# One accumulator and one tail per tile and head group: window and compressed exponentials scaled on POOL by the ratio to the selected branch's factor

## The chip, the cores and the metric

The kernel runs on one core of a Trainium2 chip. The metric is device time in microseconds (us). A core has five engines with a queue each, which run in order and wait for each other through semaphores: PE (matrix products and transposes, which write PSUM), DVE (vector), ACT (activation functions and copies), POOL (vector work without access to PSUM) and SP (which only issues DMAs here).

## The reference, cut to what matters

A decoder layer: RMS norm, one input projection, a token mixer of eight attention heads beside a short convolution, an output projection, then a squared-ReLU MLP. All of it is float32, 1024 tokens of 1024 features. The attention has three branches over the same queries, and each has its own softmax:

```
p_cmp = masked_softmax(q.k_cmp - slope * dist)   # 63 compressed keys
p_slc = masked_softmax(q.k_slc - slope * dist)   # all earlier keys (16 of 16 blocks are taken)
p_win = masked_softmax(q.k_win - slope * dist)   # the last 512 keys
o = g0 * (p_cmp @ v_cmp) + g1 * (p_slc @ v_slc) + g2 * (p_win @ v_win)   # g: sigmoid gates
```

masked_softmax divides by the row's sum. With e for the exponentials, branch b contributes f_b * (e_b @ v_b), where f_b = gate_b / sum_b is one number for each query and head.

## The kernel before

Tokens stand in 8 tiles of 128 (`tb`), heads in 2 groups (`g`) of 4. The attention stage goes over the tiles in the order 3, 2, 1, 0, 4, 5, 7, 6 and in each over both groups: 16 rounds. A round has two parts.

`scores(tb, g, ...)` makes for each head the score products (PE, two matmuls a piece, since float32 values are split in a high and a low part), adds the distance penalty and takes the maximum (DVE, from PSUM), and takes exponentials with their sums (ACT). The exponentials of a head lie in one tile `pt`: the first 640 columns hold the window's (WW = min(128 * (tb + 1), 640) of them are in use), the others the selected branch's. The compressed exponentials of all four heads lie in `pc`, 256 columns. `sm` holds the sums by branch and head, and `rr` becomes the factors f_b: a DVE product with `gates` (which holds 1 + exp(-z), the gate's reciprocal) and a reciprocal. `HEADS` is the order of the heads, and a head's place in it is `sl`.

`weigh(tb, g, ...)` returns steps, which the next round's `scores` runs between its heads (`filler`). A step is a block of 128 keys: `load` transposes the exponentials of four heads to PSUM (tile `tp`) and splits them into `ph` (ACT) and `pl` (DVE), `use` multiplies them with the values (`vs`, `vw`, or `vc` and `vco`) into an accumulator `ot`. At the last block of a branch `tail` takes the accumulator out: ACT copies it to `oTs`, PE transposes it back in four pieces into `ops`, and what follows scales it by `rr[:, b]` and adds it to `og`, a part of the tile's output row `osb`, on POOL. The branches come in the order selected (b = 1, tb + 1 blocks), window (2, at most 5 blocks), compressed (0, one block). `finish` then normalizes `osb`, transposes it (`tpo`) and makes the output projection (`wa`). The tiles `ops`, `tpo` and `wa` share one PSUM bank (tag `ms`), the accumulators two (tag `ot`).

`queries` prepares a tile's queries, with a memset and a cast into `Qz` on POOL, which the score products with the low parts need.

None of this runs in the order in which it is written. All calls are recorded as nodes of a plan, and `Plan.schedule` orders them over the whole kernel by priorities worked out from a table of costs for each engine, then issues each engine's queue in that order. Any edit so gives a new order. All instructions are issued from one helper, line 268, so the profile tells them apart by tiles.

After the attention the MLP's up and down products follow. Their first weights are prepared while the last tiles are at work.

Of the kernel before, what the change touches and what calls it, by code (L numbers as in the profile page):

```python
# [494 lines left out]
def trunk_layer(ctx, tc, x, g_mix_norm, w_in, g_q, g_k, pe_cmp, w_cmp1, b_cmp1, w_cmp2, b_cmp2,  # L495
# [182 lines left out]
    with ExitStack() as b1:  # L678
# [120 lines left out]
        for tb, ps in (a for tbs in QUADS for a in z_tokens(pieces, tbs, 280, steps, 1)):  # L799
            z = zt.tile([P, 512], F32, name="z")  # L800
            copy_act(z[:, :280], ps[:, :280])
            k_norm(z[:, 0:128], 2, kn[tb // 2][:, tb % 2, 1])
            v_split(z[:, 128:256], "w", tb)
            e = st.tile([P, 3 * H], F32, name="ge")
            nc.scalar.activation(e, z[:, 256:280], AF.Exp, scale=-1.0)
            for g in range(G):
                eg = e[:, g * 12:(g + 1) * 12].rearrange("p (i j b) -> p b j i", i=2, b=3)
                nc.vector.tensor_scalar(gates[:, tb, g].rearrange("p b (j i) -> p b j i", j=2), eg, 1.0, None,
                                        op0=ALU.add)

        pieces = w_chunk(0, 512, lo_eng=nc.vector)
        for tb, ps in (a for tbs in QUADS for a in z_tokens(pieces, tbs, 512, steps, 1)):
# [24 lines left out]
    with ExitStack() as b2:  # L837
# [92 lines left out]
        def scores(tb, g, Qt, filler):  # L930
            Qg, Qz = Qt
            W = (tb + 1) * P
            WW = min(W, 640)
            nm = st.tile([P, 3, R], F32, name="nm")
            sm = st.tile([P, 3, R], F32, name="sm")
            pc = pts[g].tile([P, R, NCMP], F32, name="pc", bufs=1)
            Ps = []
            k_w = NCMP + T + W - WW
            N = NCMP + W
            cuts = [N] if N <= 512 else [320, N] if N <= 640 else [N - 512, N] if N <= 1024 else [320, N - 512, N]  # L940
            pieces = []
            c0 = 0
            for c1 in cuts:
                parts = [] if c0 else [(0, 0, NCMP, 0)]
                o = max(c0, NCMP)
                parts.append((1, o - NCMP, c1 - o, o - c0))
                pieces.append((c0, c1 - c0, parts))
                c0 = c1
            if WW == 640:
                pieces.append((k_w + 384, 256, [(2, 384, 256, 0)]))  # L950
                pieces.append((k_w, 384, [(2, 0, 384, 0)]))
            else:
                pieces.append((k_w, WW, [(2, 0, WW, 0)]))
            banks = []
            for k, n, parts in pieces:
                m = max(n, 256)
                for bank in banks:
                    if bank[0] + m <= 512:
                        break
                else:  # L960
                    bank = [0, []]
                    banks.append(bank)
                bank[1].append((k, m, bank[0], parts))
                bank[0] += m
            dtile = {0: (d_c, 56 - 8 * tb), 2: (d_sw, 512 + 640 - WW), 1: (d_sw, T - W)}
            for sl, r in enumerate(HEADS):
                sc = -(2.0 ** -(g * R + r + 1))
                pt = pts[g].tile([P, 640 + T], F32, name="pt", bufs=R)
                Ps.append(pt)
                dst = {0: pc[:, r], 2: pt[:, 0:WW], 1: pt[:, 640:640 + W]}  # L970
                seen = set()
                for _, group in banks:
                    s_ = psS.tile([P, 512], F32, name="s_")
                    for k, m, s0, _ in group:
                        nc.tensor.matmul(s_[:, s0:s0 + m], Qg[:, r], KH[g][:, k:k + m], start=True, stop=False)
                        nc.tensor.matmul(s_[:, s0:s0 + m], Qz[:, r], KL[:, k:k + m], start=False, stop=True)
                    for k, m, s0, parts in group:
                        for b, off, n, x in parts:
                            dd, d0 = dtile[b]
                            if b == 1 and d0 + off >= 512:  # L980
                                d0 += P
                            acc = nm[:, b, sl:sl + 1]
                            nc.vector.tensor_tensor_reduce(out=dst[b][:, off:off + n], in0=s_[:, s0 + x:s0 + x + n],
                                                           in1=dd[:, d0 + off:d0 + off + n],
                                                           scale=sc, scalar=acc if b in seen else 1e20,
                                                           op0=ALU.add, op1=ALU.min, accum_out=acc)
                            seen.add(b)
                for b in (1, 2):
                    nc.scalar.activation(dst[b], dst[b], AF.Exp, bias=nm[:, b, sl:sl + 1],
                                         scale=-1.0, accum_out=sm[:, b, sl:sl + 1])  # L990
                for _ in range(-(-len(filler) // (R - sl))):
                    filler.pop(0)()
            order = "p (j i) -> p i j"
            mx = nm[:, 0].rearrange(order, j=2).unsqueeze(3).to_broadcast([P, 2, 2, NCMP])
            pv = pc.rearrange("p (i j) n -> p i j n", j=2)
            tt(nc.gpsimd, pv, mx, pv, ALU.subtract)
            nc.scalar.activation(pc, pc, AF.Exp)
            nc.vector.tensor_reduce(sm[:, 0].rearrange(order, j=2), pv, axis=AX.X, op=ALU.add)
            rr = st.tile([P, 3, R], F32, name="rr")
            nc.vector.scalar_tensor_tensor(rr, sm, 1e-30, gates[:, tb, g], op0=ALU.max, op1=ALU.mult)  # L1000
            nc.vector.reciprocal(rr, rr)
            return (Ps, pc), rr

        def queries(tb):
            Qs = []
# [57 lines left out]
    with ExitStack() as c_:  # L1063
# [15 lines left out]
        def weigh(tb, g, probs, rr, osb):  # L1079
# [15 lines left out]
            def use(ot, first, last, ph, pl, vs):  # L1095
# [3 lines left out]
                for i, v in enumerate(vs):  # L1099
                    o = ot[0][:, i * w:(i + 1) * w]  # L1100
                    nc.tensor.matmul(o, v, ph, start=first, stop=False)
                    nc.tensor.matmul(o, v, pl, start=False, stop=last)

            def tail(ot, b):
                oTs = pq.tile([P, 512], F32, name="oTs", bufs=2)
                copy_act(oTs, ot[0])
                ops = psC.tile([P, R, 2, HD], F32, name="ops", tag="ms", bufs=1)
                for r in range(R):
                    nc.tensor.transpose(ops[:, r].rearrange("p a d -> p (a d)"), oTs[:, r * P:(r + 1) * P], ident)
                t = pq.tile([P, R, 2, HD], F32, name="ot_s", bufs=2)  # L1110
                tv = t.rearrange("p (j i) a d -> p j i a d", j=2)
                if b in (0,9):
                    copy_act(t, ops)
                    tt(nc.gpsimd, tv[:, :, :, 0], tv[:, :, :, 0], tv[:, :, :, 1], ALU.add)
                    c = rr[:, b].rearrange("p (j i) -> p j i", j=2).unsqueeze(3).to_broadcast([P, 2, 2, HD])
                    tt(nc.gpsimd, tv[:, :, :, 0], tv[:, :, :, 0], c, ALU.mult)
                    tt(nc.gpsimd, og, og, tv[:, :, :, 0], ALU.add)
                    return
                c = rr[:, b].unsqueeze(2).unsqueeze(3).to_broadcast([P, R, 2, HD])
                tt(nc.vector, t, ops, c, ALU.mult)  # L1120
                if b == 1:
                    tt(nc.gpsimd, og, tv[:, :, :, 0], tv[:, :, :, 1], ALU.add)
                else:
                    for k in range(2):
                        tt(nc.gpsimd, og, og, tv[:, :, :, k], ALU.add)

            def flat(a):
                return a.rearrange("p a d -> p (a d)")
# [2 lines left out]

            def drain(n):
                while len(fifo) > n:
                    ot, first, last, hl, v, b = fifo.pop(0)
                    use(ot, first, last, *hl, v)
                    if last:
                        tail(ot, b)

            def block(ot, first, last, ins, v, b):
                hl = load(ins)  # L1140
                drain(2)
                fifo.append((ot, first, last, hl, v, b))

            def cols_of(o):
                return [p[:, o:o + P] for p in Ps]

            for b, blocks in ((1, [(cols_of(640 + j * P), [flat(V["s"][:, j, g])]) for j in range(tb + 1)]),
                              (2, [(cols_of(j * P), [flat(V["w"][:, tb + 1 - nw + j, g])]) for j in range(nw)]),
                              (0, [([flat(pc[:, 2 * i:2 * i + 2]) for i in range(2)], [v[:, g] for v in VC])])):
                ot = []  # L1150
                for i, a in enumerate(blocks):
                    steps.append(lambda a=(ot, i == 0, i == len(blocks) - 1) + a + (b,): block(*a))
            steps.append(lambda: drain(0))
            return steps

# [380 lines left out]
```

## Time and profile before

| what | value |
|---|---|
| median of 3 runs | 1266.03 us (1264.09 to 1266.17) |
| the profiled execution: time, span | 1264.1 us, 1262.3 us |
| granted PE clock | 0.999 |
| PE, DVE, ACT, POOL busy | 1234.4, 902.1, 683.1, 708.5 us |

The span is what the profiler saw between the first and the last instruction. The busy time of an engine is not what it costs: only work on the chain that ends last sets the time. In the profile, `out<-in` names an instruction by the tiles it writes and reads, and `PEld` is PE's loading of weights, which overlaps its products.

### The profile page before, as it was taken

The numbers are of one execution on the slowest core, as the hardware profiler recorded it, in microseconds if no ns is written. First come the engines' busy times: TensorE is split into PE (matmuls) and PEld (weight loads), VectorE is DVE, ScalarE is ACT, GpSimd is POOL, SyncE is SP. The second block draws the span as 40 slices with busy tenths as digits, with TensorE's granted clock in tenths as the row PEclk, the third lists the DMA queues.
The fourth block names the chain that finished last, engine by engine and source line by source line (L and its number), as shares of the span: only waits on it lengthen the run. The fifth ranks groups of instructions, "written<-read, shape, count | busy, mean of one in ns | idle before, by whom it ended". The sixth has DMA issues, their size and how long they took to land.

```text
span 1262.3 us, 18410 instructions
## 1 busy us (share of the span) xinstructions
PE 1234.4 (98%) x6170; PEld 1023.4 (81%) x6170; DVE 902.1 (71%) x1805; ACT 683.1 (54%) x1418; POOL 708.5 (56%) x631
## 2 busy tenths in 40 slices
PE   7999999999999999999999999999999999999998
PEld 6898888888878888888778888888888787888786
DVE  6367874434787888988785656566558999898874
ACT  7345552111688888887957455554435444444440
POOL 2155522121044532322687777778788989888860
PEclk9999999999999999999999999999999999999999
DMA  6253441213220100000315445354349654544413
GB/s 236 77 126 119 134 118 50 70 38 122 73 76 34 58 28 18 26 18 18 117 65 193 132 153 166 115 171 159 133 150 371 206 173 167 169 154 132 139 42 133
DMA packets 91574, 147.67 MB, mean 117 GB/s; under 512 B 10900, under 2 KB 45800, under 8 KB 91480
## 3 DMA queue, kind: packets, MB, share of 16 engines
q1 hardware_dynamic: 88408, 138.70, 33.1%
q10 hardware_dynamic: 2304, 5.24, 1.1%
q0 software_dynamic: 768, 2.56, 0.6%
q8 instruction: 49, 0.80, 0.3%
q14 instruction: 45, 0.37, 0.1%
HBM read 102.43 MB, written 44.04 MB: 116 GB/s over the span
## 4 chain that ended last, share of the span: by engine, by line
PE 87%; DMA 4%; ACT 4%; DVE 3%; issue 1%; SPq 0%; POOL 0%; ACTq 0%; DVEq 0%; POOLq 0%
PE X L268 24%; PE Z L268 16%; PE zc L268 10%; PE zp L268 8%; PE tp L268 6%; PE ot L268 5%; PE wa L268 4%; PE W L268 3%; PE wc L268 3%; DMA wu<-in_w_up_dram 2%; PE ops L268 1%; DVE we L268 1%; PE hp L268 1%; DVE y L268 1%; ACT wu L268 1%
## 5 line engine op out<-in xcount | busy, mean ns | idle before, releaser
L268 PE MATMUL X<-we,uu 128*128 128x512 f32 x720 | 179.2, 390 | 1.6 <-DVE y L268 1.5
L268 PEld LDWEIGHTS X<-we,uu 128*128 128x128 f32 x720 | 134.5, 188 | 31.5 <-ACT uu L268 2.2
L268 PE MATMUL Z<-we,uu 128*128 128x512 f32 x576 | 146.8, 391 | 0.3 <-DVE y L268 0.3
L268 ACT ACTIVATE uu<-ur 128x512 fp32r<-128x512 f32 x108 | 67.7, 633 | 127.2 <-PE X L268 57.4
L268 PEld LDWEIGHTS Z<-we,uu 128*128 128x128 f32 x576 | 107.3, 188 | 25.2 <-DVE y L268 2.1
L268 POOL TENSOR_TENSOR d<-d 128x512 f32<-128x512 f32 x64 | 97.0, 1536 | 10.0 <-DVE d L268 8.8
L268 PE MATMUL tp<-ident,pt 128*128 128x128 f32 x528 | 101.9, 273 | 0.2 <-DVE rs_t L268 0.2
L268 DVE TENSOR_TENSOR pl<-tp,ph 128x512 fp32r<-128x512 f32 (+1 forms) x148 | 94.5, 655 | 9.2 <-ACT ph L268 7.8
L268 ACT ACTIVATE pt<-pt,nm 128x640 f32<-128x640 f32 (+7 forms) x128 | 94.1, 739 | 8.4 <-DVE nm L268 7.6
L268 ACT ACTIVATE ph<-tp 128x512 fp32r<-128x512 f32 (+1 forms) x148 | 82.3, 579 | 27.9 <-PE tp L268 17.0
L268 ACT ACTIVATE w_hi<-w_raw,cols 128x128 fp32r<-128x128 f32 (+3 forms) x128 | 54.1, 488 | 67.8 <-PE zc L268 48.3
L268 DVE TENSOR_TENSOR y<-X,y 128x512 f32<-128x512 f32 x128 | 79.8, 681 | 13.7 <-PE X L268 13.0
L268 POOL TENSOR_TENSOR uu<-ur,uu 128x512 fp32r<-128x512 f32 x54 | 77.5, 1440 | 13.6 <-DVE y L268 8.8
L268 DVE TENSOR_TENSOR we<-s,we 128x512 fp32r<-128x512 f32 x42 | 40.7, 969 | 56.8 <-ACT we L268 25.4
L268 DVE SCALAR_TENSOR_TENSOR w_lo<-w_raw,cols,w_hi 128x128 fp32r<-128x128 f32 (+3 forms) x128 | 62.3, 530 | 24.4 <-ACT w_hi L268 24.3
L268 DVE TENSOR_TENSOR uu<-ur,uu 128x512 fp32r<-128x512 f32 x54 | 69.2, 1293 | 12.5 <-ACT uu L268 11.4
L268 PEld LDWEIGHTS tp<-ident,pt 128*128 128x128 f32 x528 | 67.8, 140 | 11.8 <-PE s__4915 L268 0.6
L268 DVE TENSOR_TENSOR y<-Z,y 128x512 f32<-128x512 f32 x96 | 61.3, 683 | 21.1 <-PE Z L268 21.1
L268 ACT ACTIVATE we<-wu 128x512 fp32r<-128x512 f32 x57 | 35.8, 634 | 59.8 <-PE X L268 47.8
L268 ACT ACTIVATE wu<-wu,cols 128x256 f32<-128x256 f32 x128 | 55.6, 506 | 22.5 <-DMA wu<-in_w_up_dram 22.1
L268 PE MATMUL zc<-hTl,w_hi 128*128 128x512 f32 x192 | 65.3, 389 | 0.0
L268 PE MATMUL zc<-hTh,w_lo 128*128 128x512 f32 x192 | 65.1, 390 | 0.0
(1270 smaller groups left out, 3596.9 us busy)
## 6 DMA issues: line engine op xcount, KB each, us to landing
u_d<-d SPq DMA_DIRECT2D x112, 256.0 KB, 5.5
ur<-u_d SPq DMA_DIRECT2D x108, 256.0 KB, 2.7
wu<-in_w_up_dram SPq DMA_DIRECT2D x16, 1024.0 KB, 6.1
wd<-in_w_down_dram SPq DMA_DIRECT2D x16, 1024.0 KB, 5.9
w_raw<-in_w_in_dram SPq DMA_DIRECT2D x20, 512.0 KB, 3.9
xt<-in_x_dram SPq DMA_DIRECT2D x10, 512.0 KB, 5.5
w_raw<-in_w_cmp_dram SPq DMA_DIRECT2D x8, 512.0 KB, 3.9
q_d<-qn SPq DMA_DIRECT2D x8, 512.0 KB, 2.9
```

The source lines that it names most:

```text
L268: node.do.append(lambda: getattr(engine, method)(*[real(x) for x in a], **{k: real(x) for k, x in kw.items()}))
```

## The change

There is one accumulator for all three branches, and one tail. Since only one factor can be applied at its end, that of the selected branch, the window's and the compressed exponentials are multiplied beforehand by f_2 / f_1 and f_0 / f_1. POOL does this, in place: two products on 128x4 for the ratios (`rr[:, 2]` and `rr[:, 0]`), four on a head's WW window columns, one on `pc`. The factors themselves now lie in `ra`, which takes the place of `sm`. 1 + exp(-z) is cut off at 1e20 (a second operation of the same instruction) and the sums at .5 where 1e-30 was. The blocks of the three branches form one list, the first starts the accumulator and the last ends it.

```diff
--- before.py
+++ after.py
@@ -805,8 +805,8 @@
             nc.scalar.activation(e, z[:, 256:280], AF.Exp, scale=-1.0)
             for g in range(G):
                 eg = e[:, g * 12:(g + 1) * 12].rearrange("p (i j b) -> p b j i", i=2, b=3)
-                nc.vector.tensor_scalar(gates[:, tb, g].rearrange("p b (j i) -> p b j i", j=2), eg, 1.0, None,
-                                        op0=ALU.add)
+                nc.vector.tensor_scalar(gates[:, tb, g].rearrange("p b (j i) -> p b j i", j=2), eg, 1.0, 1e20,
+                                        op0=ALU.add, op1=ALU.min)
 
         pieces = w_chunk(0, 512, lo_eng=nc.vector)
         for tb, ps in (a for tbs in QUADS for a in z_tokens(pieces, tbs, 512, steps, 1)):
@@ -963,9 +963,11 @@
                 bank[1].append((k, m, bank[0], parts))
                 bank[0] += m
             dtile = {0: (d_c, 56 - 8 * tb), 2: (d_sw, 512 + 640 - WW), 1: (d_sw, T - W)}
+            dst_w = []
             for sl, r in enumerate(HEADS):
                 sc = -(2.0 ** -(g * R + r + 1))
                 pt = pts[g].tile([P, 640 + T], F32, name="pt", bufs=R)
+                dst_w.append(pt[:, 0:WW])
                 Ps.append(pt)
                 dst = {0: pc[:, r], 2: pt[:, 0:WW], 1: pt[:, 640:640 + W]}
                 seen = set()
@@ -997,9 +999,17 @@
             nc.scalar.activation(pc, pc, AF.Exp)
             nc.vector.tensor_reduce(sm[:, 0].rearrange(order, j=2), pv, axis=AX.X, op=ALU.add)
             rr = st.tile([P, 3, R], F32, name="rr")
-            nc.vector.scalar_tensor_tensor(rr, sm, 1e-30, gates[:, tb, g], op0=ALU.max, op1=ALU.mult)
-            nc.vector.reciprocal(rr, rr)
-            return (Ps, pc), rr
+            nc.vector.scalar_tensor_tensor(rr, sm, .5, gates[:, tb, g], op0=ALU.max, op1=ALU.mult)
+            ra = sm
+            nc.vector.reciprocal(ra, rr)
+            for b in (2, 0):
+                tt(nc.gpsimd, rr[:, b], ra[:, b], rr[:, 1], ALU.mult)
+            for sl, r in enumerate(HEADS):
+                o = dst_w[sl]
+                tt(nc.gpsimd, o, o, rr[:, 2, sl:sl + 1].to_broadcast([P, WW]), ALU.mult)
+            c = rr[:, 0].rearrange(order, j=2).unsqueeze(3).to_broadcast([P, 2, 2, NCMP])
+            tt(nc.gpsimd, pv, pv, c, ALU.mult)
+            return (Ps, pc), ra
 
         def queries(tb):
             Qs = []
@@ -1099,30 +1109,19 @@
                 for i, v in enumerate(vs):
                     o = ot[0][:, i * w:(i + 1) * w]
                     nc.tensor.matmul(o, v, ph, start=first, stop=False)
-                    nc.tensor.matmul(o, v, pl, start=False, stop=last)
-
-            def tail(ot, b):
+                    nc.tensor.matmul(o, v, pl, start=False, stop=last and i == len(vs) - 1)
+
+            def tail(ot):
                 oTs = pq.tile([P, 512], F32, name="oTs", bufs=2)
                 copy_act(oTs, ot[0])
                 ops = psC.tile([P, R, 2, HD], F32, name="ops", tag="ms", bufs=1)
                 for r in range(R):
                     nc.tensor.transpose(ops[:, r].rearrange("p a d -> p (a d)"), oTs[:, r * P:(r + 1) * P], ident)
                 t = pq.tile([P, R, 2, HD], F32, name="ot_s", bufs=2)
+                c = rr[:, 1].unsqueeze(2).unsqueeze(3).to_broadcast([P, R, 2, HD])
+                tt(nc.vector, t, ops, c, ALU.mult)
                 tv = t.rearrange("p (j i) a d -> p j i a d", j=2)
-                if b in (0,9):
-                    copy_act(t, ops)
-                    tt(nc.gpsimd, tv[:, :, :, 0], tv[:, :, :, 0], tv[:, :, :, 1], ALU.add)
-                    c = rr[:, b].rearrange("p (j i) -> p j i", j=2).unsqueeze(3).to_broadcast([P, 2, 2, HD])
-                    tt(nc.gpsimd, tv[:, :, :, 0], tv[:, :, :, 0], c, ALU.mult)
-                    tt(nc.gpsimd, og, og, tv[:, :, :, 0], ALU.add)
-                    return
-                c = rr[:, b].unsqueeze(2).unsqueeze(3).to_broadcast([P, R, 2, HD])
-                tt(nc.vector, t, ops, c, ALU.mult)
-                if b == 1:
-                    tt(nc.gpsimd, og, tv[:, :, :, 0], tv[:, :, :, 1], ALU.add)
-                else:
-                    for k in range(2):
-                        tt(nc.gpsimd, og, og, tv[:, :, :, k], ALU.add)
+                tt(nc.gpsimd, og, tv[:, :, :, 0], tv[:, :, :, 1], ALU.add)
 
             def flat(a):
                 return a.rearrange("p a d -> p (a d)")
@@ -1131,25 +1130,25 @@
 
             def drain(n):
                 while len(fifo) > n:
-                    ot, first, last, hl, v, b = fifo.pop(0)
+                    ot, first, last, hl, v = fifo.pop(0)
                     use(ot, first, last, *hl, v)
                     if last:
-                        tail(ot, b)
-
-            def block(ot, first, last, ins, v, b):
+                        tail(ot)
+
+            def block(ot, first, last, ins, v):
                 hl = load(ins)
                 drain(2)
-                fifo.append((ot, first, last, hl, v, b))
+                fifo.append((ot, first, last, hl, v))
 
             def cols_of(o):
                 return [p[:, o:o + P] for p in Ps]
 
-            for b, blocks in ((1, [(cols_of(640 + j * P), [flat(V["s"][:, j, g])]) for j in range(tb + 1)]),
-                              (2, [(cols_of(j * P), [flat(V["w"][:, tb + 1 - nw + j, g])]) for j in range(nw)]),
-                              (0, [([flat(pc[:, 2 * i:2 * i + 2]) for i in range(2)], [v[:, g] for v in VC])])):
-                ot = []
-                for i, a in enumerate(blocks):
-                    steps.append(lambda a=(ot, i == 0, i == len(blocks) - 1) + a + (b,): block(*a))
+            blocks = [(cols_of(640 + j * P), [flat(V["s"][:, j, g])]) for j in range(tb + 1)]
+            blocks += [(cols_of(j * P), [flat(V["w"][:, tb + 1 - nw + j, g])]) for j in range(nw)]
+            blocks.append(([flat(pc[:, 2 * i:2 * i + 2]) for i in range(2)], [v[:, g] for v in VC]))
+            ot = []
+            for i, a in enumerate(blocks):
+                steps.append(lambda a=(ot, i == 0, i == len(blocks) - 1) + a: block(*a))
             steps.append(lambda: drain(0))
             return steps
```

How the new plan stands, at two places. POOL, tile 4, first group. Before, these are the row for the compressed scores (`pc`, subtracted from their maximum), the selected tail's add, two adds of the window's tail, and three steps of the compressed tail:

```order
L268 TENSOR_TENSOR pc<-nm,pc 128x256
L268 TENSOR_TENSOR osb<-ot_s 128x2x2x64
L268 TENSOR_TENSOR osb<-osb,ot_s 128x2x2x64 x2
L268 TENSOR_TENSOR ot_s<-ot_s 128x4x64
L268 TENSOR_TENSOR ot_s<-ot_s,rr 128x4x64
L268 TENSOR_TENSOR osb<-osb,ot_s 128x2x2x64
```

Now, from the ratios on (`rr`), for the same tile and group:

```order
L268 TENSOR_TENSOR rr<-sm,rr 128x4 x2
L268 TENSOR_TENSOR pt<-pt,rr 128x640 x4
L268 TENSOR_TENSOR pc<-pc,rr 128x256
L268 TENSOR_TENSOR osb<-ot_s 128x2x2x64
L268 TENSOR_TENSOR pc<-nm,pc 128x256
L268 COPY Qz<-Qg 64x512
```

The adds of three tails became one (`osb<-ot_s`, which belongs to an earlier round), and the ratios, four products on 640 columns and the one on `pc` stand in one piece, ahead of the next group's `pc` and `Qz`.

PE, around tile 0's last blocks. Before, from the end of a compressed branch (`vco`) on; `s_` are score products of the tile that comes next and `tpq` transposes of its queries:

```order
L268 MATMUL ot<-pl,vco 128x256
L268 MATMUL ops<-ident,oTs 128x128 x4
L268 MATMUL s__4789<-KH_2793,Qg 128x512
L268 MATMUL s__4789<-KL,Qz 128x512
L268 MATMUL tpq<-ident,qx 128x128 x3
L268 MATMUL s__4813<-KH_2793,Qg 128x384
L268 MATMUL s__4813<-KL,Qz 128x384
L268 MATMUL tpq<-ident,qx 128x128
L268 MATMUL tp<-ident,pt 128x128 x2
L268 MATMUL ops<-ident,oTs 128x128 x4
```

Now, in the second group of tile 0; the four `tp<-ident,pt` are its window's transposes, which read what POOL has scaled:

```order
L268 MATMUL tp<-ident,pt 128x128
L268 MATMUL wa<-w_hi,mh 128x512
L268 MATMUL tp<-ident,pt 128x128
L268 MATMUL wa<-w_lo,mh 128x512
L268 MATMUL s__4630<-KH_2793,Qg 128x512
L268 MATMUL tp<-ident,pt 128x128
L268 MATMUL wa<-w_hi,ml 128x512
L268 MATMUL s__4630<-KL,Qz 128x512
L268 MATMUL s__4649<-KH_2793,Qg 128x384
L268 MATMUL tp<-ident,pc 128x128
L268 MATMUL wa<-w_hi,mh 128x512
L268 MATMUL tp<-ident,pc 128x128
```

Before, four `ops` transposes stood behind each branch; now they come once a group, and between the window's transposes stand pieces of an output projection (`wa`) and score products.

## The prediction

> **What bounds the kernel now.** I read the page first: engine shares, slices of the span, and the chain that ended last.
>
> ```profile
> span 1262.3 us, 18410 instructions
> PE 1234.4 (98%) x6170; PEld 1023.4 (81%) x6170; DVE 902.1 (71%) x1805; ACT 683.1 (54%) x1418; POOL 708.5 (56%) x631
> ...
> PE   7999999999999999999999999999999999999998
> ...
> DVE  6367874434787888988785656566558999898874
> ACT  7345552111688888887957455554435444444440
> POOL 2155522121044532322687777778788989888860
> PEclk9999999999999999999999999999999999999999
> ...
> PE 87%; DMA 4%; ACT 4%; DVE 3%; issue 1%; SPq 0%; POOL 0%; ACTq 0%; DVEq 0%; POOLq 0%
> ```
>
> PE is busy in every slice at full clock and carries 87% of the chain; POOL carries none of it. Next the attention stage, the only one that the change touches. The first matmul into an accumulator (view of the tile `ot`) and the last output projection `wa` (chain in order of time) give its ends, so I asked for the busy times of 340 to 640 us (columns: length, then busy time and count of PE, PEld, DVE, ACT, POOL).
>
> ```profile
> L268 PE MATMUL ot<-ph,vs x72: 388/477/504, 339.1 to 609.9; 128*128 128x512 f32 x72
> ```
> ```profile
> 636.26 0.93 PE wa L268 x4
> ```
> ```profile
> 340.00:440.00 100.00, 96.62 (x603) 80.92 (x602) 83.29 (x292) 86.93 (x226) 45.65 (x68) 1.00 0.15 51
> 440.00:540.00 100.00, 97.83 (x619) 83.59 (x618) 88.54 (x291) 82.87 (x174) 33.73 (x52) 1.00 0.08 28
> 540.00:640.00 100.00, 97.66 (x604) 81.27 (x603) 83.11 (x212) 84.00 (x173) 44.41 (x50) 1.00 0.14 48
> sum 300.00, PE 292.12 PEld 245.79 DVE 254.95 ACT 253.80 POOL 123.79; mean PE 97.37 PEld 81.93 DVE 84.98 ACT 84.60 POOL 41.26
> ```
>
> PE is idle for 7.9 us of 300, DVE and ACT for some 45 each, POOL for 176. So PE work taken out here should count nearly in full, as long as nothing new makes PE wait.
>
> The 240 to 260 us stretch is an unbroken run of wide matmuls, and weight loads fill 16.57 of its 20 us, 83%; in the stage they fill 82%. So the stage is nearly as dense by that measure too.
>
> ```profile
> 240.00:260.00 20.00, 20.00 (x90) 16.57 (x89) 7.47 (x9) 4.35 (x6) 8.25 (x6) 1.00 0.25 79
> ```
>
> [...]
>
> **Removed: two of three tails in each of 16 groups** (8 tiles by 2 head groups). The view of the tile `ops` counts them, the one of `ot` the copies, and the chain in order of time (start, duration, piece) gives the rate at which PE issues transposes.
>
> ```profile
> L268 PE MATMUL ops<-ident,oTs x192: 270/272/330, 345.1 to 619.7; 128*128 128x128 f32 x192
> L268 DVE TENSOR_TENSOR ot_s<-ops,rr x32: 675/686/692, 348.9 to 618.5; 128x512 f32<-128x512 f32 x32
> L268 ACT ACTIVATE ot_s<-ops x16: 577/600/663, 354.8 to 620.4; 128x512 f32<-128x512 f32 x16
> ```
> ```profile
> L268 ACT ACTIVATE oTs<-ot x48: 579/599/631, 344.4 to 618.5; 128x512 f32<-128x512 f32 x48
> ```
> ```profile
> 411.77 0.44 PE ops L268 x4
> ...
> 431.08 2.77 PE wa L268 x12
> ...
> 614.43 1.58 ACT wu L268 x4
> ...
> 624.86 2.80 ACT wu L268 x7
> ```
>
> The 272 ns of one transpose overlap the next; four in a row take 0.44 us of the chain, so one costs 0.11 us of PE. 192 become 64: 128 x 0.11 = **14.1 us of PE less**. The matmuls into the accumulator stay as many; only start and stop flags differ. DVE loses 16 x 0.686 = 11.0 us (the window's scaling), ACT 32 x 0.599 + 16 x 0.600 = 28.8 us. Both were under PE, so I cost these at nothing by themselves; they thin out the queues in which the split of transposed exponentials (`ph`, `pl`) stands.
>
> What PE waited for on the old tails is this (engine and tile, releaser: us in total, times, longest):
>
> ```profile
> PEld ops L268 <- ACT oTs L268: 3.9, 10, 0.6
> ...
> PEld tpo L268 <- ACT ot_s L268: 1.7, 3, 1.0
> ...
> PE tpo L268 <- ACT ot_s L268: 1.3, 3, 0.8
> ...
> PE ops L268 <- ACT oTs L268: 1.0, 4, 0.2
> ...
> PE tp L268 <- DVE rr L268: 0.8, 1, 0.8
> ```
>
> Of the 4.9 us on `oTs`, two thirds of the tails go: -3.3 us (bounds 0 and -4.9: a single tail may also be later). The 3.0 us before `tpo` end with ACT's copy of the compressed tail and three POOL steps behind it; the new tail has one DVE scaling and one POOL add. I take half, -1.5 us (bounds 0 and -3.0). Each wait may be counted on both PE rows, so these are upper figures.
>
> **Added and moved on POOL.** Rows of POOL's groups in 340 to 640 us (busy, mean ns):
>
> ```profile
> L268 POOL TENSOR_TENSOR osb<-osb,ot_s 128x256 f32<-128x256 f32 x48 | 37.9, 790 | 23.0 <-DVE ot_s L268 19.6 <-DVE rr L268 1.3
> ...
> L268 POOL TENSOR_TENSOR ot_s<-ot_s 128x256 f32<-128x256 f32 x16 | 11.7, 734 | 3.7 <-ACT ot_s L268 3.5
> L268 POOL TENSOR_TENSOR ot_s<-ot_s,rr 128x256 f32<-128x256 f32 x16 | 9.8, 614 | 0.7
> L268 POOL TENSOR_TENSOR pc<-nm,pc 128x256 f32<-128x256 f32 x15 | 9.2, 615 | 61.3 <-DVE nm L268 48.3 <-DVE rs_t L268 12.7
> ...
> L268 POOL TENSOR_TENSOR wu<-wu 128x512 f32<-128x512 f32 x5 | 6.4, 1285 | 0.2
> L268 POOL TENSOR_TENSOR y<-y,t 128x512 f32<-128x512 f32 x3 | 5.3, 1757 | 0.0
> L268 POOL TENSOR_TENSOR ri<-rs_t,mhalf 128x1 f32<-128x1 f32 x8 | 4.9, 612 | 13.5 <-DVE rs_t L268 12.0 <-DVE rr L268 1.5
> ```
>
> Gone are the first three: 59.4 us. Added per group: two products on 128x4, four on the window's 128xWW, one on `pc`. The row nearest in kind is 128x256 times a broadcast factor, 0.615 us; the step from 256 to 512 columns (734 to 1285 ns) is 2.15 ns a column. So 128 columns 0.34 us, 256 0.615, 384 0.89, 512 1.17, 640 1.44. No row shows 640: proportion to the broadcast row gives 1.54, the slowest row, 1757 ns, 1.44 x 1757/1285 = 1.97; with a start-up of 0.18 us taken off and 1.7 ns a column, 1.27. I take 1.44, the step between two rows of this trace. WW is 128, 256, 384, 512 in tiles 0 to 3 and 640 in the other four: 64 products, 8 x (0.34 + 0.615 + 0.89 + 1.17 + 4 x 1.44) = 70.2 us. `pc`: 16 x 0.615 = 9.8. The 32 small products have no row: 0.61 us (a power on one column, a heavier operation) is above, 0.1 below; I take 0.2, near the start-up, 6.4 us. Together 86 us against 59 removed: POOL goes from 124 to about 151 us of the stage. It stays the idlest engine, so its load by itself costs nothing.
>
> [...]
>
> **The new wait.** The factor needs all three sums of all four heads, so the window's transposes, which used to wait only for their exponentials, now stand behind this chain, and so do the ones of the compressed branch:
>
> ```profile
> L268 ACT ACTIVATE pc<-pc x16: 405/419/436, 329.1 to 600.3; 128x256 f32<-128x256 f32 x16
> L268 DVE TENSOR_REDUCE sm<-pc x16: 407/414/420, 329.7 to 602.2; 128x4 f32<-128x256 f32 x16
> ...
> L268 DVE SCALAR_TENSOR_TENSOR rr<-sm,gates x16: 159/168/690, 332.8 to 604.2; 128x12 f32<-128x12 f32 x16
> L268 DVE RECIPROCAL rr<-rr x16: 211/224/229, 333.0 to 604.9; 128x12 f32<-128x12 f32 x16
> ```
>
> From the last sum: 0.17 + 0.22 on DVE, 2 x 0.2 and four products on POOL: 0.8 us plus 1.4, 2.5, 3.6, 4.7 in tiles 0 to 3 and 5.8 in the larger, so 2.2, 3.3, 4.4, 5.5 and 6.6 us. Behind the waiting transposes on PE stand whatever the planner put there; behind the products on POOL stand the next group's `pc` subtraction and the `Qz` casts, which the next scores need. Cover: the group's own selected blocks come first, and one is four transposes and two matmuls of 0.23 (2.77/12), 0.90 us; there are tb + 1 of them. Own cover alone leaves short 1.3, 1.5, 1.7 and 1.9 us in tiles 0 to 3, and 2.1, 1.2, 0.3, 0 in 4 to 7; twice that, for two groups: 12.8 + 7.2 = 20.0 us. That is the upper bound. The lower is 0: the order quoted ahead shows, in tile 0, output-projection and score matmuls in just that gap, and POOL's products directly behind the ratios. The nearest case in the trace is the old compressed transposes, which hung on the same sums with little behind them to cover: PE's row for that wait (`tp` on `rr`, above) is 0.8 us in the whole stage. I lie nearer to that and take +3 us.
>
> **Sum**, against the profiled execution (1264.1 us, span 1262.3): -14.1 - 3.3 - 1.5 + 3.0 = -15.9, so 1248.2. The median of the runs is 1266.03, 1.9 above that execution: 1250.1, say **1250**. With the bounds: PE's work and all its 7.9 us of idle time gone is -22.0, that is 1244; all 20 us of new waits, no wait saved, is +5.9, that is 1272.
>
> **Rivals.**
> - *New waits take much of it.* Some tiles lack cover, most likely 0 to 3, where 12.8 us are at stake: with a third of the saved waits, -14.1 - 1.6 + 6 to 12.8 gives -9.7 to -2.9, 1256 to 1263. For it: ACT at 87% in 340 to 440 us, so exponentials come late there. Against: the planner orders around it.
> - *Slower: POOL's scaling is held back by DVE.* If each product ran at the 1757/1285 of the slowest POOL row, four on 640 columns would be 7.9 us, the chain 8.7, and own cover would be short by 1.8, 2.4, 3.0 and 3.6 us in tiles 0 to 3 and 4.2, 3.3, 2.4 and 1.5 in 4 to 7, 44 us over both groups. With two thirds of that uncovered: -14.1 - 4.8 + 29.6 = +10.7, 1277. It decides from 19 us of new waits, 1.2 us in each group. Against: DVE's commonest instruction here does not slow, `pl` below.
>
> ```profile
> L268 DVE TENSOR_TENSOR pl<-tp,ph x129: 408/685/694, 345.9 to 599.5; 128x512 fp32r<-128x512 f32 x115, 128x256 fp32r<-128x256 f32 x14
> ```
>
>   Its 685 to 694 ns at 512 columns hold whatever POOL does, for it reads PSUM for one of its inputs, as the score instructions do. [...]
> - *More than the sum.* ACT and DVE, 28.8 and 11 us lighter, also end PE's short waits: -20 to -24, 1242 to 1246.
> - *That it does not do what it says* is excluded for the counts: the order has 64 `ops` transposes. That the gain is given back after the stage I count in the first rival: ACT is on the chain between 614 and 628 us (`wu` above), but 28.8 us lighter ahead of that.
>
> **How the numbers follow.** Likeliest case 0.70 (1246 to 1256), first rival 0.12, slower rival 0.08, more than the sum 0.10. The range from 1244 to 1260 leaves out the slower rival, the upper half of the first and the far end of the last, nearly 2 in 10. A measurement here tells about 0.2%, 2.5 us, from no change; between 1263.5 and 1268.6 I see 0.05, above 0.07, so faster 0.88.
>
> **What would show it.** Right: 64 `ops` transposes, the output projection of the last tile some 15 us earlier, POOL near 150 us in the stage, four products of about 5.8 us in the larger tiles, and few waits of PE on POOL's `pt`. Wrong: PE rows that wait for `pt` from POOL for over 6 us in total, or a POOL product of 640 columns near 2 us. What would make the time wrong even so is PE idle time elsewhere, since every queue is put in a new order.

## The result and the profile after

| kernel | median | ratio to before, 95% interval |
|---|---|---|
| before (same comparison) | 1265.30 us | |
| changed | 1243.98 us (1243.12 to 1246.11, 5 runs) | 0.9837 [0.9823, 0.9852] |

The change makes the kernel 1.63% faster, 20.6 us by the ratio. The forecast was 15.9 us less and 1250 us. The median stands at the low end of the range, 1244 us, below the likeliest case (1246 to 1256 us) and where the rival "more than the sum" had it, with a chance of 0.10. The profiled execution after took 1246.11 us, 18.0 less than the profiled one before, and was the longest of its five.

The page after, rows as shown of before:

```profile
span 1244.2 us, 18122 instructions
...
PE 1217.6 (98%) x6042; PEld 1009.8 (81%) x6042; DVE 890.1 (72%) x1789; ACT 659.2 (53%) x1370; POOL 726.9 (58%) x663
...
PE   7999999999999999999999999999999999999998
...
PEclk9999999999999999999999999999999999999999
...
PE 86%; DMA 6%; DVE 4%; ACT 2%; issue 2%; POOL 0%; SPq 0%; DVEq 0%; ACTq 0%; POOLq 0%
```

PE has 128 instructions less and is as full as before. POOL, with more work, still has no share of the chain. The tile `ops` confirms one tail a group (192 transposes and 32 scalings before):

```profile
L268 PE MATMUL ops<-ident,oTs x64: 270/272/327, 356.3 to 603.6; 128*128 128x128 f32 x64
L268 DVE TENSOR_TENSOR ot_s<-ops,sm x16: 676/685/692, 357.3 to 605.1; 128x512 f32<-128x512 f32 x16
```

I measure the attention stage from the first matmul into `ot` to the last output projection `wa`: 339.1 to 637.9 us before, 341.5 to 619.3 after, so 298.8 and 277.8 us. Whole microseconds of that stretch, before and then after (length, busy time of PE, PEld, DVE, ACT, POOL):

```profile
339.00:638.00 299.00, 291.12 (x1817) 244.91 (x1816) 254.33 (x794) 253.62 (x572) 121.86 (x167) 1.00 0.12 43
```
```profile
342.00:619.00 277.00, 271.39 (x1677) 228.98 (x1677) 240.75 (x776) 229.50 (x523) 133.44 (x191) 1.00 0.14 46
```

The stage is 21 us shorter, and PE's idle time in it fell from 7.9 to 5.6 us. In the second stretch stand 140 PE instructions less, 128 of the tails and 12 others: some lie in the parts of a microsecond at the edges, and a little of the MLP's early work moved behind the stage.

What POOL was given (groups by shape, busy and mean ns):

```profile
L268 POOL TENSOR_TENSOR pt<-pt,rr 128x640 f32<-128x640 f32 x32 | 39.1, 1255 | 0.0
...
L268 POOL TENSOR_TENSOR pc<-pc,rr 128x256 f32<-128x256 f32 x16 | 9.8, 615 | 0.0
...
L268 POOL TENSOR_TENSOR pt<-pt,rr 128x512 f32<-128x512 f32 x8 | 9.1, 1165 | 0.0
...
L268 POOL TENSOR_TENSOR pt<-pt,rr 128x384 f32<-128x384 f32 x8 | 6.4, 830 | 0.0
...
L268 POOL TENSOR_TENSOR rr<-sm,rr 128x4 f32<-128x4 f32 x32 | 5.7, 202 | 34.4 <-DVE sm L268 25.5 <-ACT ph L268 7.5 <-DVE nm L268 1.2
...
L268 POOL TENSOR_TENSOR pt<-pt,rr 128x256 f32<-128x256 f32 x8 | 4.7, 615 | 0.0
...
L268 POOL TENSOR_TENSOR pt<-pt,rr 128x128 f32<-128x128 f32 x8 | 3.0, 397 | 0.0
```

One of the 64 products ran long. The tile's view gives its 2022 ns, and the other seven of that shape took 1037 to 1047 ns. In order of time (start, duration), it began while a long DVE instruction was at work, one with no input in PSUM:

```profile
L268 POOL TENSOR_TENSOR pt<-pt,rr x64: 391/1244/2022, 334.7 to 590.0; 128x640 f32<-128x640 f32 x32, 128x512 f32<-128x512 f32 x8, 128x384 f32<-128x384 f32 x8, 128x256 f32<-128x256 f32 x8
```
```profile
358.26 2.02 POOL L268 TENSOR_TENSOR pt<-pt,rr 128x512 f32<-128x512 f32 x1
```
```profile
358.03 1.35 DVE L268 SCALAR_TENSOR_TENSOR w_lo<-w_raw,cols,w_hi 128x1024 fp32r<-128x1024 f32 x1
```

And what PE waited for in 340 to 640 us (PE's weight loads first, then its products):

```profile
PEld ot L268 <- DVE pl L268: 1.7, 3, 0.9
PEld tp L268 <- POOL pt L268: 1.6, 5, 0.6
...
PEld tpo L268 <- POOL osb L268: 0.8, 3, 0.3
```
```profile
PE tp L268 <- POOL pt L268: 0.3, 1, 0.3
```

The waits on `oTs` are no longer among the larger ones. The new wait, on POOL's `pt`, is 1.6 us in five places (the 0.3 us of the products can be part of it).

### The profile page after: what moved, and what is told of

Read it like the earlier page. It is cut to its first block, busy times and chain, and to the rows that moved or that the text cites. A ratio compares the mean times of both kernels' runs of the same rounds, so it can differ in the third digit from the quotient of the medians.

```text
span 1244.2 us, 18122 instructions
## 1 busy us (share of the span) xinstructions
PE 1217.6 (98%) x6042; PEld 1009.8 (81%) x6042; DVE 890.1 (72%) x1789; ACT 659.2 (53%) x1370; POOL 726.9 (58%) x663
## 4 chain that ended last, share of the span: by engine, by line
PE 86%; DMA 6%; DVE 4%; ACT 2%; issue 2%; POOL 0%; SPq 0%; DVEq 0%; ACTq 0%; POOLq 0%
PE X L268 23%; PE Z L268 16%; PE zc L268 11%; PE zp L268 8%; PE tp L268 6%; PE ot L268 4%; PE wa L268 4%; PE W L268 4%; PE wc L268 3%; DMA wu<-in_w_up_dram 2%; PE hp L268 1%; DVE y L268 1%; DVE we L268 1%; DMA ur<-u_d 1%; ACT ph L268 1%
## 5 line engine op out<-in xcount | busy, mean ns | idle before, releaser
L268 PEld LDWEIGHTS tp<-ident,pt 128*128 128x128 f32 x528 | 68.4, 140 | 14.1 <-POOL pt L268 1.6
L268 DVE TENSOR_TENSOR y<-Z,y 128x512 f32<-128x512 f32 x96 | 61.3, 683 | 20.4 <-PE Z L268 20.4
L268 DVE SCALAR_TENSOR_TENSOR d<-d 128x512 f32<-128x512 f32 x48 | 67.0, 1398 | 0.8
```

What stands on the lines that cost most here:

```text
L268: node.do.append(lambda: getattr(engine, method)(*[real(x) for x in a], **{k: real(x) for k, x in kw.items()}))
```

## Experiments

All ratios are to the kernel before, run on the same chip (1263.6 to 1263.8 us there); a difference to the changed kernel is the difference of two ratios (its own, 0.9837, is that of the result) times 1263.7 us, with an error of some 2.5 us, for e2 3.5 and for e4 4.4. Theories: A, the gain is PE's removed work and a few of its waits. B, it is the lighter ACT and DVE. C, it is an accident of the new order. D, the chain on POOL still costs.

### e1, e2, e3, e4: one part undone, order planned anew

e1:
```diff
-                for r in range(R):
+                for r in 3 * [*range(R)]:
                     nc.tensor.transpose(ops[:, r]...
```


> The changed kernel, with each of the 16 tails transposing its accumulator back three times instead of once into the same tile, so that PE has its 128 transposes again and nothing else comes back. Theory A (the gain is PE work, 128 x 0.11 us, plus some waits): 14 us slower than the changed kernel, 1258 us, ratio to before about 0.994. Rival B (the gain comes from fewer waits and lighter ACT and DVE queues, PE's share was slack): less than 5 us slower, under 1249 us, ratio below 0.987.

Measured 1263.26 us, 0.9995 [0.9982, 1.0008]: 20.0 us slower than the changed kernel, where A said 14 and B less than 5. B's claim that PE had slack falls; the 6 us above A are open here.

e2:
```diff
-                copy_act(oTs, ot[0])
+                for _ in range(4):
+                    copy_act(oTs, ot[0])
```


> The changed kernel, with each of the 16 tails copying the accumulator four times instead of once: 48 copies of 0.60 us, the 28.8 us that the change took from ACT, come back and PE's work does not. Theory A: within 2 us of the changed kernel, 1244 to 1246 us, ratio about 0.984. Rival B (ACT's relief is the part of the gain beyond 14.1 us): 4 to 7 us slower, 1248 to 1251 us, ratio 0.987 to 0.989.

Measured 1253.40 us, 0.9921 [0.9897, 0.9945]: 10.6 us slower. That is more than even B said (7 at most), by about the error of this run. Its stage, with 9.8 us of PE idle instead of 5.6:

```profile
338.00:621.00 283.00, 273.21 (x1670) 229.21 (x1670) 242.80 (x775) 250.06 (x571) 131.48 (x191) 0.99 0.13 45
```

e3:
```diff
-            for b in (2, 0):
+            for b in (0,):
                 tt(nc.gpsimd, rr[:, b], ra[:, b], rr[:, 1], ALU.mult)
-            for sl, r in enumerate(HEADS):
-                o = dst_w[sl]
-                tt(nc.gpsimd, o, o, rr[:, 2, sl:sl + 1]...
...
+            for b, blocks in ((2, win), (1, sel)):   # sel holds the compressed block too
```


> Half of the change: only the compressed branch goes into the selected branch's accumulator, the window keeps its own accumulator, tail and factor, and comes first. 64 transposes go instead of 128, and POOL gets the 16 products on pc but none on the window. Theory A: half of the PE work, -7.0 us, and half of the saved waits, -2 to -3: 1256 us, ratio 0.992 to 0.993. Rival C (the gain is an accident of the new order, not of the work): anything between 1240 and 1265 without relation to 7 us.

Measured 1257.86 us, 0.9957 [0.9945, 0.9969]: 5.4 us faster than before, some 4 less than A said and near to a quarter of the whole gain, for half of the removed PE work. On its page PE's busy time is 6.2 us less than before (1228.2 against 1234.4), near to the 7.0 of 64 transposes, and PE's idle time, span less busy time, is 0.8 more (28.7 against 27.9): the waits that A counted as saved do not show on it.

e4:
```diff
-            for b in (2, 0):
-                tt(nc.gpsimd, rr[:, b], ra[:, b], rr[:, 1], ALU.mult)
-            for sl, r in enumerate(HEADS):
-                ...
-            tt(nc.gpsimd, pv, pv, c, ALU.mult)
```


> The changed kernel without the ratios and without the products on the window's and the compressed exponentials: these branches enter with the wrong factor. It takes away the whole new chain on POOL, 86 us of it. Theory A (the new wait is nearly covered): 0 to 3 us faster than the changed kernel, 1241 to 1244 us, ratio 0.981 to 0.984. Rival D (POOL's chain still costs): 5 us faster or more, under 1239 us, ratio below 0.979.

Measured 1250.60 us, 0.9907 [0.9875, 0.9939]: with 78 us of POOL's work taken away (62.3 + 9.8 + 5.7 in the rows above) it is 8.8 us slower. Neither theory allows that; the new order seems to cost more than the work saved. So these four runs mix two things, the work and the plan, and the next ones part them.

### f1, f2, f4, g1: the same edits in a frozen order

A node of the plan got a count; the planner sees the kernel as it was, and only when it issues does it run the node's instruction `rep` times (0 leaves it out). Apart from these instructions all queues stand as in the kernel that they come from.

```diff
-                for f in n.do:
+                for f in n.rep * n.do:
                     f()
...
+                plan.rep = 3        # f1: around the ops transposes; f2: 4 around copy_act(oTs, ...)
                                     # f4: 0 around ratios and products; g1: 0 around tail() where b != 1
```

f1:

> The 128 transposes put back as in the run e1, but into the changed kernel's own order: the planner sees the changed kernel, and each `ops` transpose is then issued three times in its place. All queues stand as in the changed kernel. Theory A (PE work, 0.11 us each): 14 to 15 us slower than the changed kernel, ratio to before 0.994 to 0.996. Theory C (a new order by itself moves the time by several us, and that made e1 20 us slower): the same 14 us here, so the rest of e1's 20 is the order. Rival B (PE had slack): under 7 us, ratio below 0.989.

Measured 1256.35 us, 0.9952 [0.9938, 0.9965]: 14.5 us slower than the changed kernel. 128 transposes at 0.11 us are 14.1. PE stays as full as it was, 5.4 us idle:

```profile
341.00:631.00 290.00, 284.63 (x1812) 243.79 (x1811) 243.30 (x777) 231.89 (x523) 133.83 (x192) 1.00 0.13 44
```

So PE's work counts in full in this order, and the other 5.5 us of e1, which issues the same instructions, were its order.

f2:

> The 28.8 us of ACT put back as in e2, in the changed kernel's own order: each copy of the accumulator is issued four times in its place. Theory C (e2's 10 us were mostly its new order): 0 to 3 us slower than the changed kernel, ratio 0.984 to 0.986. Rival B (ACT's relief is worth 5 us or more): ratio 0.988 or higher.

Measured 1263.50 us, 1.0001 [0.9992, 1.0009]: 20.7 us slower, all of the gain. I had expected 3 at most; by its letter this is rival B's case. The stage's row, and what PE waited for in it:

```profile
338.00:636.00 298.00, 277.61 (x1684) 230.99 (x1683) 243.61 (x780) 256.86 (x572) 132.43 (x192) 0.99 0.13 43
```
```profile
PEld ops L269 <- ACT oTs L269: 9.8, 7, 2.1
PEld ot L269 <- ACT ph L269: 5.2, 5, 2.0
PEld tp L269 <- ACT Qg L269: 3.7, 3, 1.8
```

PE is idle for 20.4 us instead of 5.6. The three copies more stand for 1.8 us in front of each tail's transposes (`oTs`) and in front of everything behind them on ACT (`ph`, `Qg`), and PE's own order has nothing to put there. ACT is busy for only 86% of the stage and yet this work is paid for. But the run does not price what the change took from ACT: the old tails never held four copies in a row, so it adds load and a longer tail at once.

f4:

> The changed kernel in its own order without the ratios and the products on the window's and the compressed exponentials (these branches enter with the wrong factor). It takes away the new chain on POOL and nothing else. Theory A (the chain is nearly covered): 0 to 3 us faster than the changed kernel, ratio 0.981 to 0.984; with theory C the 7 us that e4 lost against the changed kernel were its order. Rival D (the chain still costs): 5 us faster or more, ratio below 0.980.

Measured 1242.38 us, 0.9832 [0.9819, 0.9846]: 0.6 us faster than the changed kernel, less than the error. POOL's work in the stage falls from 133.4 to 63.8 us, and the other engines' work hardly moves:

```profile
338.00:616.00 278.00, 272.32 (x1688) 230.39 (x1686) 241.88 (x781) 230.06 (x524) 63.75 (x87) 1.00 0.14 46
```

The whole scaling is covered to within the error of 2.5 us, and D's 5 us or more falls. (The order is one that was laid out around the chain; what that costs, no run prices.) The 9.5 us of difference between e4 and f4, which issue the same instructions, are the order alone. Part of where e4 loses them is at the end of the stage (waits from 598 to 625 us, then two stretches of 8 us; the granted clock is the number before the DMA share):

```profile
PEld wa L268 <- ACT mh L268: 1.7, 1, 1.7
PEld tpo L268 <- POOL osb L268: 1.5, 1, 1.5
...
PEld ops L268 <- ACT oTs L268: 1.0, 1, 1.0
```
```profile
596.00:604.00 8.00, 4.87 (x31) 3.46 (x29) 8.00 (x11) 8.00 (x20) 4.74 (x4) 1.00 0.46 142
604.00:612.00 8.00, 7.09 (x32) 6.05 (x33) 6.03 (x9) 6.90 (x16) 7.92 (x7) 0.79 0.00 0
```

The last tile's tail runs there with too little beside it: PE is idle for 3.1 of 8 us, and in the next 8 us it gets 0.79 of its clock.

g1:

> The kernel before in its own order, but the tails of the window and of the compressed branch are left out (their copies, transposes, scalings and adds; these two branches then miss in the output). Nothing is added and nothing is moved: 128 transposes, 32 ACT copies of the accumulator, 16 copies and 16 scalings of the transposed tile, 64 POOL adds and 16 products less. Theory A: 14.1 us of PE work and about 5 us of waits, 18 to 20 us faster than before, ratio 0.984 to 0.986. Theory C with a lucky order of the changed kernel: only about 14 us here, ratio 0.989, and the rest of its gain came from the order.

Measured 1255.67 us, 0.9940 [0.9927, 0.9952]: only 7.6 us faster than before, and both theories said more. The stage is 10.8 us shorter (340.9 to 628.9 us), and PE is idle for 9.0 us, more than before in a shorter stretch:

```profile
341.00:629.00 288.00, 279.00 (x1687) 231.08 (x1686) 243.87 (x778) 231.76 (x524) 63.69 (x88) 1.00 0.13 44
```

In the old order the removed work buys about half of its own length. That order was made to fill PE around the old tails; with them gone PE probably reaches other work sooner than ACT and DVE have it ready, but that is not shown. On the pages, of 14.1 us only 11.3 show as less busy time of PE (1223.1 against 1234.4), and 2.7 come back as idle time (30.6 against 27.9), 1.1 of them in the stage. The 28.8 us less on ACT, which this run has too, show no gain of their own.

### p1 to p4: the same work in other orders

```diff
 # p1 on the changed kernel, p3 on the one before: POOL products with a broadcast factor
-            c = .15 + n * .00213
+            c = .185 + n * .00168 if names_bc(a) else .15 + n * .00213
 # p2 on the changed kernel, p4 on the one before
-    LINK = .05
+    LINK = .07
```


> The changed kernel with another order and the same work: in the planner's table a POOL product with a broadcast factor costs 0.185 us and 1.68 ns a column (about what the runs show) where it cost 0.15 and 2.13. Theory A (the gain is the removed work): within 3 us of the changed kernel, ratio 0.981 to 0.986. Theory C (the changed kernel's order is a lucky one; e4 and e1 lost 5 to 9 us by their orders alone): 4 us slower or more, ratio 0.987 to 0.992.

> The changed kernel with a second other order and the same work: the planner counts 0.07 us where it counted 0.05 for the hop from one engine to another. Theory A: ratio 0.981 to 0.986. Theory C: 0.987 to 0.992.

> The kernel before with the planner's price for broadcast products on POOL as in p1: the same work in another order. Theory A: within 3 us of before, ratio 0.998 to 1.002. Theory C (orders differ by 5 to 9 us for the same work, whichever kernel it is): ratio off 1 by 0.004 or more, to either side.

> The kernel before with the hop priced as in p2: the same work in another order. Theory A: ratio 0.998 to 1.002. Theory C: off 1 by 0.004 or more. The mean of before, p3 and p4 against the mean of the changed kernel, p1 and p2 gives what the change is worth over orders: theory A 18 us or more, theory C 10 to 15.

| kernel | median | ratio | span, PE busy (first rows of its page) |
|---|---|---|---|
| before | | 1 | 1262.3, 1234.4 us |
| p3, before | 1265.17 us | 1.0012 [1.0002, 1.0023] | 1263.0, 1234.6 us |
| p4, before | 1265.24 us | 1.0009 [0.9999, 1.0019] | 1262.6, 1232.3 us |
| changed | | 0.9837 [0.9823, 0.9852] | 1244.2, 1217.6 us |
| p1, changed | 1245.84 us | 0.9852 [0.9837, 0.9867] | 1244.8, 1216.7 us |
| p2, changed | 1242.11 us | 0.9823 [0.9808, 0.9838] | 1238.1, 1213.6 us |

The means over three orders each are 0.9837 for the changed kernel and 1.0007 for the one before: 0.0170, 21.5 us. Theory C would have had the changed kernel fall back and the kernel before scatter; neither did. The orders are close to each other, though: with the two sequences of PE's queue matched by tile names, p1 and p2 keep about 97 and 95% of the changed kernel's order, p3 and p4 93 and 91% of the one before, while e4 keeps 90% of f4's and e1 77% of f1's. So what these four exclude is that a small change of order loses the gain, not that a far one could.

The last column says where the gain stands. On the mean of three pages PE's busy time falls from 1233.8 to 1216.0 us, 17.8 less, and its idle time from 28.9 to 26.4, 2.5 less. p2 is the fastest kernel of the study, but its interval overlaps that of the changed kernel, so I don't call it better. PE's idle time in the stage is 5.3 us in p2 and 8.8 in p3, as in the kernels that they come from (5.6 and 7.9):

```profile
338.00:615.00 277.00, 271.66 (x1683) 229.91 (x1682) 240.68 (x779) 229.63 (x524) 134.11 (x191) 1.00 0.13 46
```
```profile
339.00:639.00 300.00, 291.17 (x1809) 244.88 (x1808) 256.10 (x793) 252.30 (x571) 119.48 (x166) 1.00 0.12 42
```

## Why the prediction was right, and where not

- **PE's work, -14.1 us: right.** f1 measures 14.5 in the changed kernel's order.
- **POOL's price: right in kind, too high.** 1.255 us for 640 columns, where I took 1.44 and had 1.27 as the lowest bound. So POOL's work in the stage came to 133 us, not the 150 that I gave as a sign of being right. From 256 to 640 columns it is 1.67 ns a column: the form with a start-up of 0.18 and 1.7 ns was nearly the one. The 64 products took 62.3 us, not 70.2; the small ones 0.20 us each, as taken.
- **New waits, +3 us: too high.** 1.6 us of PE rows name `pt`, and f4 prices the whole chain at 0.6 us. Both the rivals in which the scaling takes the gain back fall with it. The products on 640 columns did not run long beside DVE, 1.255 us on the mean. What the slower rival describes seems to happen, but only once in 64: the product of 2.02 us that began during `w_lo`. The kernel before shows the same: its adds on `osb` took 0.74 us on the median, and each of the seven above 0.8 us (1.05 to 1.59) began during a DVE instruction on 512 columns or more with no input in PSUM, three of them during a `w_lo`; the other 57 took at most 0.75 us, and none of them began during one. The reason that I gave for `pl`, that it reads PSUM, fits that trace: on 512 columns `pl` took 0.62 to 0.69 us and `y<-X,y`, which reads PSUM too, 0.67 to 0.69, with POOL at work or not, while `uu<-ur,uu`, with no input in PSUM, took 0.68 to 0.69 with POOL idle and 0.68 to 1.79 beside it, 1.44 on the median.
- **The saved waits, -4.8 us: with the new ones near the sum.** Together the wait terms are -1.8 us, and PE's idle time fell by 2.5 on the mean of three orders. Each term by itself is less sure. In the rows the waits on `oTs` go from 4.9 to 0.2 us where I had taken off 3.3, but others grow (`ot` on DVE's `pl`, 0.3 to 1.7).
- **The sum fell short by 4.7 us (15.9 against 20.6), and the cause is open.** What is missing stands not in idle time but in PE's busy time, which fell by 17.8 us, 3.7 more than 128 transposes at 0.11 us. No run says which products ran faster, or why. The rival "more than the sum" named the right time, but its reason, short waits of PE that end, would show as idle time and does so only for the 2.5 us. That the range held the result rests in part on luck.
- **Lighter ACT and DVE, costed at nothing: not settled.** The reason that I gave was too simple. The cover that I named, PE itself, hides ACT's busy time but not its delay: with 28.8 us of ACT back in the tails the time rises by 10.6 us if the order is planned for it (e2) and by 20.7 if it isn't (f2). How much of that is ACT's load, how much the 1.8 us longer tail and how much e2's order is open. What the relief itself was worth neither run says, and g1, which has it too, shows no gain from it.
- **"The removed work counts nearly in full": not in the old order.** g1 shows 7.6 us for the tails' removal there. The changed kernel has 13 us more; its new order is the likely reason, but it also has one accumulator in place of three, and no run parts the two. The prediction did not see that it had to count on a new order.
- **Reordering as what could make it wrong** was rightly named, but not sized: 5.5 us (e1 against f1) and 9.5 us (e4 against f4) where the work changed, and within 2 us of the original for four small changes of the planner's prices.

## What to carry to other kernels

In a kernel whose PE is full, take work off PE even at the price of more work on an idle engine: the 78 us that POOL was given cost 0.6 us here, less than the error, since PE had other work beside nearly all of its chains. Where in-order queues are laid out by a planner, an edit may pay only in part until it is planned anew (7.6 us in the old order, 20.6 in the new), and a part of an edit must be measured with the order frozen, or its order is measured instead. ACT, busy for 83% of the stage, was not free either: 28.8 us more on it in the tails, in front of a full PE, cost 20.7 us in the changed kernel's own order (f2) and 10.6 in a new one (e2).

## What the hardware showed that I had not expected

In e4 PE idled for 3.1 us between 596 and 604 us, in gaps of up to 1.5 us, and the granted clock of the 8 us that followed was 0.79; the same instructions in f4's order kept 1.00. Taken closer, the clock stood at half for 3.41 us, and in the 3.41 us before that PE was busy for 47% of the time (length, then busy time of PE; the clock is the number before the DMA share):

```profile
602.66:606.07 3.41, 1.60 (x7) 1.20 (x8) 3.41 (x4) 3.41 (x9) 3.41 (x3) 1.00 0.00 0
606.07:609.48 3.41, 3.41 (x14) 2.87 (x13) 2.92 (x6) 2.71 (x6) 3.41 (x4) 0.50 0.00 0
```

If PE's gaps brought the half clock on, they cost a second time, by an estimate of 1.7 us, half of the 3.41. e2, e3 and f2 show the same 3.41 us at half clock behind their last tail, after 3.41 us in which PE was busy for 47, 38 and 44%; before, the changed kernel and f4 do not, and f4's PE was busy for 82% of 602.66 to 606.07 us. No single gap in e4 was longer than 1.5 us. PE's busy time alone does not account for the half clock: e1 and e3 each have such a stretch near 287 us too, behind one in which the profile shows PE busy throughout. So what sets it off is not shown.
